# Moving the low-part subtraction of the second expert table's activations from GpSimd to VectorE

## The chip, the cores and the metric

The kernel runs on one core of a Trainium2 chip. The metric is the device time of one execution in microseconds (us), read as the median of several runs; smaller is better. The engines are named as the profile names them: PE (TensorE, matrix products; PEld is its weight load), DVE (VectorE), ACT (ScalarE), POOL (GpSimd) and SP (SyncE, which issues the bulk loads).

## What is computed

Two transformer blocks on 256 tokens of width 2048. The change lies in the last stage of the second block, a mixture of 16384 single-row experts:

```
act = gelu(einsum('cd,ckd->ck', hc, u_tab[ec])) * gate      # 128 picked experts a token
out = einsum('ck,ckd->cd', act, v_tab[ec])                  # sum of the picked rows of v_tab
return rmsnorm(x + out)
```

`u_tab` and `v_tab` are the first and the second table, 16384 rows of 2048 float32 values each.

## The kernel before

Almost all products are made in float32r from a high and a low part: with a = ah + al and v = vh + vl, a product is ah·vh + ah·vl + al·vh, three matmuls that accumulate in one PSUM bank. Where a table is streamed, `_stream` (lines 231 to 255) loads a piece, ACT rounds it to its high part (`hi`, line 251) and DVE subtracts that from the piece (`lo`, line 254). All matmuls go through `_mm`, line 259.

The expert stage is `_peer`. Its first part multiplies the tokens with every row of the first table and leaves, for every expert and token, the gated activation, zero where the expert was not picked. It lies in SBUF as 128 blocks (`sa` holds blocks 0 to 51, `sb` the rest), each 128 experts by 256 tokens. The ungated activations are also written to DRAM, into `wide`, beside 512 columns of the second table.

The second part, lines 1581 to 1604, is the stage of the change. It handles the 2048 output columns in two ways at once:

- Columns 0 to 1535 are done as a dense product, block by block. For each of the 128 blocks, ACT makes the high part of the activations (`ah`, line 1586) and an engine subtracts to get the low part (`al`, line 1587). The block's piece of the second table arrives in two loads, 512 KB and 256 KB, and is split into three groups of 512 columns (`hi` on ACT, `lo` on DVE). PE then does 18 matmuls a block: three groups, two halves of the tokens, and the three products hi·ah, lo·ah and hi·al, into six PSUM banks.
- Columns 1536 to 2047 are done by gathering. For each of the 128 picks of a token, and for each half of the tokens, `_row_sums` issues an indirect DMA on POOL (`vrow`, line 1454, 256 in all) that fetches, per token, 512 table values and 128 activations. DVE picks the right activation and multiplies it with the gate (line 1468, a SCALAR_TENSOR_TENSOR on 128x128 whose sum goes to `pval`), then adds the weighted row to two further PSUM banks (line 1475, a SCALAR_TENSOR_TENSOR on 128x512).

So one block asks of DVE three `lo`, two line-1468 and two line-1475 instructions; of ACT three `hi` and one `ah`; of POOL two gathers and one `al`; of PE 18 matmuls.

The order of instructions on each engine is made by a scheduler when the kernel is built, from the dependencies and from its own estimates; each engine then runs its list strictly in order. Buffers limit how far an engine can run ahead: `ah` and `al` have three each, `hi` and `lo` four each, `vrow` ten (five picks). An instruction that writes a buffer waits until the last reader of its former content is done.

Of the kernel before, what the change touches and what calls it, by code (L numbers as in the profile page):

```python
# [10 lines left out]
F32 = mybir.dt.float32  # L11
# [4 lines left out]
OP = mybir.AluOpType  # L16
# [214 lines left out]
def _stream(k, src, total):  # L231
    nc = k.nc
    for r in range(0, total, k.rk * 256):
        n = min(total - r, k.rk * 256)
        if k.raw2 is not None and n <= 512:
            raw = k.raw2.tile([128, 512], F32, name="raw")
        else:
            raw = k.raw.tile([128, k.rk * 256], F32, name="raw")
        small = k.n == 0
        if not small:  # L240
            load = nc.sync.dma_start(raw[:, :n], src[:, r:r + n])
            if k.side:
                _after(k, nc.sync.dma_start(*k.side.pop(0)), load)
        step = 512 if small else k.gr
        for a in range(0, n, step):
            m = min(step, n - a)
            if small:
                nc.sync.dma_start(raw[:, a:a + m], src[:, r + a:r + a + m])
            hi = k.hi.tile([128, k.gr], F32R, name="hi")
            lo = k.lo.tile([128, k.gr], F32R, name="lo")  # L250
            nc.scalar.activation(hi[:, :m], raw[:, a:a + m], AF.Copy)  # L251
            k.n += 1
            eng = nc.gpsimd if k.pool_lo and k.n % k.pool_lo == 0 else nc.vector
            k.low = eng.tensor_tensor(lo[:, :m], raw[:, a:a + m], hi[:, :m].bitcast(F32), op=OP.subtract)  # L254
            yield hi, lo, m


def _mm(k, out, lhsT, rhs, start=False, stop=False):
    return k.nc.tensor.matmul(out, lhsT, rhs, start=start, stop=stop, skip_group_check=True)  # L259
# [38 lines left out]
def _rsqrt(k, pool, v, n, tag):  # L298

    nc = k.nc  # L300
    y = pool.tile([128, n], F32, name="rs_y" + tag, tag="rs_y" + tag)
    t = pool.tile([128, n], F32, name="rs_t" + tag, tag="rs_t" + tag)
    yi = y.bitcast(I32)
    nc.vector.tensor_single_scalar(yi, v.bitcast(I32), 1, op=OP.logical_shift_right)
    nc.vector.tensor_scalar(yi, yi, -1, 0x5F3759DF, op0=OP.mult, op1=OP.add)
    for _ in range(3):
        nc.vector.tensor_tensor(t, y, y, op=OP.mult)
        nc.vector.scalar_tensor_tensor(t, t, -0.5, v, op0=OP.mult, op1=OP.mult)
        nc.vector.scalar_tensor_tensor(y, t, 1.5, y, op0=OP.add, op1=OP.mult)
    return y  # L310
# [1134 lines left out]
def _row_sums(k, picks, wide, rows, acc):  # L1445


    nc = k.nc
    ready = []

    def fetch(j):
        for t in range(2):
            r = rows.tile([128, DS + 128], F32, name="vrow")
            nc.gpsimd.indirect_dma_start(r, None, wide, bass.IndirectOffsetOnAxis(ap=picks.row[:, t, j:j + 1], axis=0),  # L1454
                                         element_offset=128 * t)
            ready.append(r)

    ahead = RB // 2 - 1
    for j in range(ahead):
        fetch(j)  # L1460
    for j in range(128):
        got = []
        for t in range(2):
            r = ready.pop(0)
            p, v = (r[:, DS:], r[:, :DS]) if t else (r[:, :128], r[:, 128:])

            w = picks.val[:, t, j:j + 1]
            i = nc.vector.scalar_tensor_tensor(p, p, picks.gate[:, t, j:j + 1], k.ident, op0=OP.mult, op1=OP.mult, accum_out=w)  # L1468
            _after(k, i, k.low)
            got.append((v, w))  # L1470
        for t, (v, w) in enumerate(got):
            if j == 0:
                i = nc.vector.tensor_scalar(acc[t], v, w, None, op0=OP.mult)
            else:
                i = nc.vector.scalar_tensor_tensor(acc[t], v, w, acc[t], op0=OP.mult, op1=OP.add)  # L1475
            _after(k, i, k.low)
        if j + ahead < 128:
            fetch(j + ahead)
        yield


def _peer(k, I, O, hctx, pers, sa, tctx, t1, x3n, wide, rb):
    nc, tc = k.nc, k.tc
# [20 lines left out]
    with ExitStack() as sctx:  # L1504
# [69 lines left out]
        with ExitStack() as c:  # L1574
            pso = c.enter_context(tc.tile_pool(name="pso", bufs=1, space=bass.MemoryType.PSUM))
            v2 = c.enter_context(tc.tile_pool(name="v2", bufs=3, side="right"))
            k.raw2 = c.enter_context(tc.tile_pool(name="raw2", bufs=6, side="right"))
            out = [[pso.tile([128, 512], F32, name=f"o{t}{q}") for q in range(4)] for t in range(2)]
            rows = c.enter_context(tc.tile_pool(name="vr", bufs=RB, side="right"))
            sums = _row_sums(k, picks, wide, rows, [out[t][3] for t in range(2)])  # L1580
            taken = 0
            for e in range(128):
                src = S_[0][:, e] if e < SA else S_[1][:, e - SA]
                ah = v2.tile([128, 256], F32R, name="ah")
                al = v2.tile([128, 256], F32R, name="al")
                nc.scalar.activation(ah, src, AF.Copy)
                nc.gpsimd.tensor_tensor(al, src, ah.bitcast(F32), op=OP.subtract)  # L1587
                for g, (vh, vl, _) in enumerate(_stream(k, I["v"][e], D - DS)):
                    for t in range(2):
                        ts = slice(t * 128, t * 128 + 128)  # L1590
                        for n, (s_, m_) in enumerate(((ah, vh), (ah, vl), (al, vh))):
                            _mm(k, out[t][g], s_[:, ts], m_, start=e == 0 and n == 0, stop=e == 127 and n == 2)
                if e == 24:

                    xn = [S_[0][:, 8 * t:8 * t + 8].rearrange("p a b -> p (a b)").rearrange("p (a b) -> p a b", b=512) for t in range(2)]
                    for t in range(2):
                        nc.scalar.dma_start(xn[t], x3n[t].rearrange("p (a b) -> p a b", b=512))
                while taken < 128 and taken * 122 < (e - 2) * 128:
                    next(sums, None)
                    taken += 1  # L1600
            for _ in sums:
                pass
            k.raw2 = None
            sctx.close()
            fin = c.enter_context(tc.tile_pool(name="fin", bufs=1))
            nf = fin.tile([128, 4, 512], F32, name="nf")
            nc.scalar.dma_start(nf.rearrange("p a b -> p (a b)"), I["normf"].to_broadcast([128, D]))
            for t in range(2):
                ss = fin.tile([128, 4], F32, name=f"ss{t}")
                sq = fin.tile([128, 512], F32, name=f"fsq{t}")  # L1610
                for q in range(4):
                    nc.vector.tensor_tensor(xn[t][:, q], xn[t][:, q], out[t][q], op=OP.add)
                    nc.scalar.activation(sq, xn[t][:, q], AF.Square, accum_out=ss[:, q:q + 1])
                v = fin.tile([128, 1], F32, name=f"fv{t}")
                nc.vector.tensor_reduce(v, ss, axis=AX.X, op=OP.add)
                nc.vector.tensor_scalar(v, v, 1.0 / D, EPS, op0=OP.mult, op1=OP.add)
                r = _rsqrt(k, fin, v, 1, f"f{t}")
                for q in range(4):
                    nc.vector.scalar_tensor_tensor(xn[t][:, q], xn[t][:, q], r, nf[:, q], op0=OP.mult, op1=OP.mult)
                    (nc.sync if q % 2 else nc.scalar).dma_start(O["out"][t * 128:t * 128 + 128, q * 512:q * 512 + 512], xn[t][:, q])  # L1620
# [47 lines left out]
def _second_block(k, I, O, hctx, cctx, x2d, sqa):  # L1668
# [20 lines left out]
    with ExitStack() as c:  # L1689
# [30 lines left out]
        _natural(k, xl, f, x3n)  # L1720
    cctx.close()
    _peer(k, I, O, hctx, pers, sa, tctx, t1, x3n, wide, rb)
    ctx.close()

# [42 lines left out]
```

## Time and profile before

| what | value |
| --- | --- |
| median of 3 runs | 3388.03 us (3386.93 to 3388.34) |
| the profiled execution's own time | 3391.95 us |
| its span in the profile | 3390.1 us |
| mean granted clock of PE | 0.983 |
| busy share of the span | PE 97%, DVE 76%, ACT 46%, POOL 26% |
| the stage of the change | 2778.76 to 3375.58 us of the span, first to last matmul |

The profile gives times from the start of the span. In a timeline view a row has the start, the duration, the engine, the line, the operation, what it writes and reads, and how many consecutive instructions were merged (x3); in brackets stands the time for which the engine sat idle before it and what it waited for. Rows of one engine can overlap by a few hundredths of a microsecond, since an instruction's end overlaps the next one's start; the distance between starts is therefore the cost of an instruction in a full engine. PE rows overlap much more, and the distance of starts is the only measure there.

### The profile page before, as it was taken

To read this page: it belongs to the slowest core of one execution; us is meant where nothing else is said; L and a number is where in the kernel's file an instruction comes from. 1 tells how busy PE (TensorE), PEld (TensorE's weight loads), DVE (VectorE), ACT (ScalarE), POOL (GpSimd) and SP (SyncE) were. 2 spreads that over 40 slices of the span, in tenths; PEclk is the share of its full clock that TensorE was granted. 3 is DMA by queue.
4 is the path that set the end of the run, shared out by engine and by line. 5 is a ranking of instruction groups with operands and counts; after the bars stand their busy time and mean duration, and the time that the engine had idled before them with its cause. 6 is when DMAs were issued, how large, how long until landed. Compare 5 with 4: busy or idle time off the path is not lost.

```text
span 3390.1 us, 65776 instructions
## 1 busy us (share of the span) xinstructions
PE 3272.4 (97%) x25018; PEld 3050.2 (90%) x25018; DVE 2571.7 (76%) x5477; ACT 1572.2 (46%) x2810; POOL 866.4 (26%) x1036
## 2 busy tenths in 40 slices
PE   8999899999999979999999999999999999999998
PEld 8999899999999979888879999999999996777776
DVE  8775587777744468788865778776777869999999
ACT  5444444444433345555454544444444444444444
POOL 3110210000000055454410000001223226666663
PEclk9999999999999979999989999999999999999999
DMA  5545455555555568653126566666566679999996
GB/s 194 168 156 174 131 168 186 178 184 187 182 180 186 172 248 286 194 169 100 52 81 200 181 200 195 190 200 188 179 176 183 180 218 335 316 320 324 317 324 225
DMA packets 239341, 680.46 MB, mean 201 GB/s; under 512 B 58160, under 2 KB 88752, under 8 KB 214832
## 3 DMA queue, kind: packets, MB, share of 16 engines
q1 hardware_dynamic: 167824, 560.53, 51.0%
q0 software_dynamic: 20480, 83.90, 7.5%
q10 hardware_dynamic: 50720, 31.82, 3.2%
q8 instruction: 196, 3.21, 0.4%
q14 instruction: 121, 0.99, 0.1%
HBM read 649.55 MB, written 60.16 MB: 209 GB/s over the span
## 4 chain that ended last, share of the span: by engine, by line
PE 71%; DVE 17%; DMA 7%; issue 3%; ACT 1%; POOL 1%; SPq 0%; DVEq 0%; ACTq 0%; POOLq 0%
PE acc L259 57%; DVE lo L254 6%; PE held L259 5%; DMA raw<-in_v 4%; DVE vrow L1468 3%; DVE o L1475 2%; PE o L259 2%; PE ps_g L259 2%; PE R L259 1%; DVE hl L349 1%; DVE ltmp L1038 1%; PE ps_p L259 1%; DMA wide<-in_vs 1%; DMA s<-g 1%; PE ps_S L259 1%
## 5 line engine op out<-in xcount | busy, mean ns | idle before, releaser
L251 ACT ACTIVATE hi<-raw 128x512 fp32r<-128x512 f32 (+1 forms) x1582 | 1147.4, 732 | 1365.3 <-PE acc L259 864.7
L254 DVE TENSOR_TENSOR lo<-raw,hi 128x512 fp32r<-128x512 f32 (+1 forms) x1492 | 1229.1, 841 | 574.2 <-ACT hi L251 561.5
L259 PE MATMUL acc<-hh,hi 128*128 128x256 f32 x4928 | 1406.6, 286 | 22.2 <-ACT hh L348 13.4
L259 PE MATMUL acc<-hh,lo 128*128 128x256 f32 x4928 | 1407.1, 286 | 13.3 <-DVE lo L254 13.1
L259 PE MATMUL acc<-hl,hi 128*128 128x256 f32 x4928 | 1400.2, 284 | 7.5 <-DVE hl L349 7.4
L259 PEld LDWEIGHTS acc<-hh,hi 128*128 128x128 f32 x4928 | 938.4, 190 | 26.0 <-ACT hh L348 14.2
L259 PEld LDWEIGHTS acc<-hh,lo 128*128 128x128 f32 x4928 | 932.0, 189 | 18.6 <-DVE lo L254 16.8
L259 PEld LDWEIGHTS acc<-hl,hi 128*128 128x128 f32 x4928 | 938.1, 190 | 11.0 <-DVE hl L349 9.7
L259 PE MATMUL o<-lo,ah 128*128 128x512 f32 x768 | 314.4, 410 | 13.2 <-DVE lo L254 7.2
L1454 POOL DMA_INDIRECT vrow<-wide,prow x256 | 269.6, 1053 | 198.2 <-DVE o L1475 146.9
L259 PE MATMUL o<-hi,al 128*128 128x512 f32 x768 | 304.3, 398 | 5.4 <-POOL al L1587 5.4
L259 PE MATMUL o<-hi,ah 128*128 128x512 f32 x768 | 222.7, 399 | 9.3 <-ACT hi L251 8.3
L259 PEld LDWEIGHTS o<-lo,ah 128*128 128x128 f32 x768 | 144.6, 188 | 85.4 <-DVE lo L254 55.1
L259 PE MATMUL acc<-gh,lo 128*128 128x256 f32 x704 | 199.2, 283 | 0.0
L259 PE MATMUL acc<-gl,hi 128*128 128x256 f32 x704 | 199.2, 283 | 0.0
L259 PE MATMUL acc<-gh,hi 128*128 128x256 f32 x704 | 199.2, 283 | 0.0
L259 PEld LDWEIGHTS o<-hi,ah 128*128 128x128 f32 x768 | 143.7, 189 | 49.4 <-ACT hi L251 14.7
L1525 POOL TENSOR_SCALAR oh<-iota,sel 128x128 f32<-128x128 f32 x128 | 92.9, 736 | 352.7 <-PE ps_g L259 323.7
L259 PEld LDWEIGHTS o<-hi,al 128*128 128x128 f32 x768 | 145.8, 190 | 36.6 <-POOL al L1587 5.8
L1475 DVE SCALAR_TENSOR_TENSOR o<-vrow,pval,o 128x512 f32<-128x512 f32 x254 | 178.3, 744 | 0.0
L254 POOL TENSOR_TENSOR lo<-raw,hi 128x512 fp32r<-128x512 f32 (+1 forms) x90 | 132.4, 1473 | 157.5 <-ACT hi L251 144.7
L1468 DVE SCALAR_TENSOR_TENSOR vrow<-vrow,pgate,ident 128x128 f32<-128x128 f32 x256 | 163.8, 675 | 2.4 <-DMA vrow<-wide,prow 2.4
(476 smaller groups left out, 4320.4 us busy)
## 6 DMA issues: line engine op xcount, KB each, us to landing
raw<-in_u SPq DMA_DIRECT2D x256, 512.0 KB, 4.5
raw<-in_w_up SPq DMA_DIRECT2D x85, 1024.0 KB, 5.1
raw<-in_v SPq DMA_DIRECT2D x128, 512.0 KB, 5.9
raw<-in_w_in SPq DMA_DIRECT2D x43, 1024.0 KB, 5.1
raw<-in_w_dn SPq DMA_DIRECT2D x40, 1024.0 KB, 4.9
wide<-in_vs SPq DMA_DIRECT2D x64, 512.0 KB, 6.0
raw<-in_v SPq DMA_DIRECT2D x128, 256.0 KB, 6.0
raw<-in_w_rkv SPq DMA_DIRECT2D x48, 512.0 KB, 3.8
```

What stands on the lines that cost most here:

```text
L251: nc.scalar.activation(hi[:, :m], raw[:, a:a + m], AF.Copy)
L254: k.low = eng.tensor_tensor(lo[:, :m], raw[:, a:a + m], hi[:, :m].bitcast(F32), op=OP.subtract)
L259: return k.nc.tensor.matmul(out, lhsT, rhs, start=start, stop=stop, skip_group_check=True)
L349: k.nc.vector.scalar_tensor_tensor(lo, t, scale, hi.bitcast(F32), op0=OP.mult, op1=OP.subtract)
L1038: nc.vector.tensor_tensor(tmp[:, :, 0:t], tt[:, :, 0:t], lq[:, 0:t, t][:, None, :].to_broadcast([128, 8, t]), op=OP.mult)
L1454: nc.gpsimd.indirect_dma_start(r, None, wide, bass.IndirectOffsetOnAxis(ap=picks.row[:, t, j:j + 1], axis=0), element_offset=128 * t)
L1468: i = nc.vector.scalar_tensor_tensor(p, p, picks.gate[:, t, j:j + 1], k.ident, op0=OP.mult, op1=OP.mult, accum_out=w)
L1475: i = nc.vector.scalar_tensor_tensor(acc[t], v, w, acc[t], op0=OP.mult, op1=OP.add)
L1525: eng.tensor_scalar(aj, iota, sel[:, 0, t:t + 1], None, op0=OP.is_equal)
```

## The change

One word: the subtraction that makes `al` is issued on DVE, not on POOL. Nothing else of the text changes.

```
@@ -1584,7 +1584,7 @@
                 ah = v2.tile([128, 256], F32R, name="ah")
                 al = v2.tile([128, 256], F32R, name="al")
                 nc.scalar.activation(ah, src, AF.Copy)
-                nc.gpsimd.tensor_tensor(al, src, ah.bitcast(F32), op=OP.subtract)
+                nc.vector.tensor_tensor(al, src, ah.bitcast(F32), op=OP.subtract)
```

The scheduler answers with other lists on four engines. On DVE, in the middle of the stage, the list of one block reads before as follows (`vrow_37796` and `vrow_37798` are the two gathered pieces of one pick, the `lo` are the three groups of one table block):

```order
L1468 SCALAR_TENSOR_TENSOR vrow_37796,pval_22307<-vrow_37796,pgate_22306,ident_58 128x128
L1468 SCALAR_TENSOR_TENSOR vrow_37798,pval_22307<-vrow_37798,pgate_22306,ident_58 128x128
L1475 SCALAR_TENSOR_TENSOR o03_34500<-vrow_37796,pval_22307,o03_34500 128x512
L1475 SCALAR_TENSOR_TENSOR o13_34504<-vrow_37798,pval_22307,o13_34504 128x512
L254 TENSOR_TENSOR lo_37991<-raw_37988,hi_37990 128x512
L254 TENSOR_TENSOR lo_38001<-raw_37988,hi_38000 128x512
L254 TENSOR_TENSOR lo_38013<-raw_38010,hi_38012 128x512
```

and with the change:

```order
L1468 SCALAR_TENSOR_TENSOR vrow_37796,pval_22307<-vrow_37796,pgate_22306,ident_58 128x128
L1468 SCALAR_TENSOR_TENSOR vrow_37798,pval_22307<-vrow_37798,pgate_22306,ident_58 128x128
L1587 TENSOR_TENSOR al_38031<-sb_27699,ah_38030 128x256
L1475 SCALAR_TENSOR_TENSOR o03_34500<-vrow_37796,pval_22307,o03_34500 128x512
L1475 SCALAR_TENSOR_TENSOR o13_34504<-vrow_37798,pval_22307,o13_34504 128x512
L254 TENSOR_TENSOR lo_37991<-raw_37988,hi_37990 128x512
L254 TENSOR_TENSOR lo_38001<-raw_37988,hi_38000 128x512
L254 TENSOR_TENSOR lo_38013<-raw_38010,hi_38012 128x512
```

The `al` of the block after the one whose `lo` follow stands between the two kinds of gather work; the rest keeps its order.

On POOL, at the start of the stage (the `sb` rows are the end of the part before, the DMA rows are the gathers), the list reads before:

```order
L1567 TENSOR_TENSOR sb<-sb,gtmp 128x512 x2
L1587 TENSOR_TENSOR al<-sa,ah 128x256 x3
L1567 TENSOR_TENSOR sb<-sb,gtmp 128x512
L1454 DMA vrow<-wide,prow 128x640 x10
L1587 TENSOR_TENSOR al<-sa,ah 128x256 x3
L1454 DMA vrow<-wide,prow 128x640 x4
L1587 TENSOR_TENSOR al<-sa,ah 128x256
L1454 DMA vrow<-wide,prow 128x640 x2
```

and with the change:

```order
L1567 TENSOR_TENSOR sb<-sb,gtmp 128x2x252
L1567 TENSOR_TENSOR sb<-sb,gtmp 128x512 x3
L1454 DMA vrow<-wide,prow 128x640 x256
L1763 UNCONDITIONAL_BRANCH
```

The `al` of blocks 3 to 5 stood behind ten gathers; now the 256 gathers follow each other alone.

On ACT, the `ah` of a block normally stands right before the three `hi` of the block ahead of it. At block 30 (counted from 0) the list before has two `ah` in a row, the second two blocks ahead:

```order
L1586 ACTIVATE ah_35852<-sa_20983 128x256
L1586 ACTIVATE ah_35898<-sa_20983 128x256
L251 ACTIVATE hi_35812<-raw_35810 128x512
L251 ACTIVATE hi_35822<-raw_35810 128x512
L251 ACTIVATE hi_35834<-raw_35832 128x512
```

and with the change:

```order
L1586 ACTIVATE ah_35852<-sa_20983 128x256
L251 ACTIVATE hi_35812<-raw_35810 128x512
L251 ACTIVATE hi_35822<-raw_35810 128x512
L251 ACTIVATE hi_35834<-raw_35832 128x512
L1586 ACTIVATE ah_35898<-sa_20983 128x256
```

The second `ah` has moved behind the three `hi`. The list before has eight blocks with an `ah` two ahead (12, 14, 19, 30, 50, 71, 91 and 111), the list with the change three (11, 14 and 19).

## Rows read from the trace of the kernel before

**Rows 1.** The page, part 1: busy time, share and instructions of each engine.

```profile
PE 3272.4 (97%) x25018; PEld 3050.2 (90%) x25018; DVE 2571.7 (76%) x5477; ACT 1572.2 (46%) x2810; POOL 866.4 (26%) x1036
```

**Rows 2.** Windows: length, busy of PE, PEld, DVE, ACT, POOL, clock, DMA share, GB/s.

```profile
2810.00:3350.00 540.00, 520.01 (x2107) 387.21 (x2106) 535.65 (x1081) 256.12 (x468) 344.80 (x359) 1.00 0.93 322
...
3050.00:3060.00 10.00, 10.00 (x44) 8.02 (x44) 9.67 (x20) 5.81 (x11) 7.31 (x8) 1.00 1.01 381
3060.00:3070.00 10.00, 10.00 (x45) 8.02 (x44) 10.00 (x20) 4.87 (x10) 6.57 (x8) 1.00 0.95 333
```

**Rows 3.** Timeline of DVE, 3055.5 to 3065: start, duration, engine, line, operation.

```profile
3055.56 1.22 DVE L1468 SCALAR_TENSOR_TENSOR vrow<-vrow,pgate,ident 128x128 f32<-128x128 f32 x1
...
3056.72 0.34 DVE L1468 SCALAR_TENSOR_TENSOR vrow<-vrow,pgate,ident 128x128 f32<-128x128 f32 x1
...
3058.31 1.88 DVE L254 TENSOR_TENSOR lo<-raw,hi 128x512 fp32r<-128x512 f32 x3
3060.11 1.23 DVE L1468 SCALAR_TENSOR_TENSOR vrow<-vrow,pgate,ident 128x128 f32<-128x128 f32 x1
```

**Rows 4.** Timeline of POOL beside it.

```profile
3055.88 0.75 POOL L1587 TENSOR_TENSOR al<-sb,ah 128x256 fp32r<-128x256 f32 x1
...
3059.27 1.14 POOL L1454 DMA_INDIRECT vrow<-wide,prow  x1 [0.30 <-DVE lo L254]
```

**Rows 5.** Timeline of DVE, 3036 to 3048.

```profile
3039.89 0.34 DVE L1468 SCALAR_TENSOR_TENSOR vrow<-vrow,pgate,ident 128x128 f32<-128x128 f32 x1
...
3040.43 1.40 DVE L1475 SCALAR_TENSOR_TENSOR o<-vrow,pval,o 128x512 f32<-128x512 f32 x2
...
3043.56 0.34 DVE L1468 SCALAR_TENSOR_TENSOR vrow<-vrow,pgate,ident 128x128 f32<-128x128 f32 x1
...
3047.23 0.34 DVE L1468 SCALAR_TENSOR_TENSOR vrow<-vrow,pgate,ident 128x128 f32<-128x128 f32 x1
```

**Rows 6.** Timeline of POOL beside it.

```profile
3040.87 0.75 POOL L1587 TENSOR_TENSOR al<-sb,ah 128x256 fp32r<-128x256 f32 x1
3041.78 1.49 POOL L1454 DMA_INDIRECT vrow<-wide,prow  x1 [0.16 <-issue]
```

**Rows 7.** Timeline of PE, 3040 to 3062: the same matmul of three blocks in a row.

```profile
3043.28 0.40 PE L259 MATMUL o<-lo,ah 128*128 128x512 f32 x1
...
3047.49 0.40 PE L259 MATMUL o<-lo,ah 128*128 128x512 f32 x1
...
3051.71 0.40 PE L259 MATMUL o<-lo,ah 128*128 128x512 f32 x1
```

**Rows 8.** Groups by form on DVE: count, busy us, mean ns, idle before.

```profile
L711 DVE TENSOR_TENSOR gl<-y,gh 128x256 fp32r<-128x256 f32 x44 | 18.4, 418 | 0.0
L349 DVE SCALAR_TENSOR_TENSOR hl<-x,cols,hh 128x256 fp32r<-128x256 f32 x64 | 44.1, 721 | 2.9 <-ACT hh L348 2.9
```

**Rows 9.** Timeline of PE: start of the stage.

```profile
2778.76 0.47 PE L259 MATMUL o<-hi,ah 128*128 128x512 f32 x1 [0.93 <-DVE gtmp L1561]
...
2783.32 1.26 PE L259 MATMUL o<-hi,ah 128*128 128x512 f32 x4 [1.53 <-ACT hi L251]
...
2801.68 2.93 PE L259 MATMUL o<-hi,al 128*128 128x512 f32 x6 [5.40 <-POOL al L1587]
```

**Rows 10.** Timeline of PE: end of the stage.

```profile
3375.18 0.40 PE L259 MATMUL o<-hi,al 128*128 128x512 f32 x1
```

**Rows 11.** Waits, 2778 to 2815: who waited for whom, us, times, longest.

```profile
DVE vrow L1468 <- DMA vrow<-wide,prow: 2.4, 3, 1.2
```

**Rows 12.** Timeline of PE, 2858 to 2872, where an `ah` is two ahead.

```profile
2864.04 0.39 PE L259 MATMUL o<-hi,al 128*128 128x512 f32 x1
2865.28 1.26 PE L259 MATMUL o<-hi,ah 128*128 128x512 f32 x4 [0.86 <-ACT hi L251]
```

**Rows 13.** Waits, 2800 to 3300.

```profile
ACT hi L251 <- DMA raw<-in_v: 3.4, 5, 0.8
```

More of the change, by code (lines that the diff above doesn't have):

```diff
@@ L1586, in _peer @@
                 nc.scalar.activation(ah, src, AF.Copy)
-                nc.gpsimd.tensor_tensor(al, src, ah.bitcast(F32), op=OP.subtract)
+                nc.vector.tensor_tensor(al, src, ah.bitcast(F32), op=OP.subtract)
                 for g, (vh, vl, _) in enumerate(_stream(k, I["v"][e], D - DS)):
```

## The prediction

> **What bounds the kernel now.** The page's first part says PE 97% and DVE 76% over the whole span [rows 1]. That average hides the stage in question, so the next view is the windows. From 2810 to 3350 us, DVE is busy 535.65 of 540 us, against 76% overall, and PE 520 of 540 [rows 2]. PE's busy time is no proof that PE is full, since its rows overlap; its pace must be taken from the distance of starts. So the reader should ask of this stage: how long is a block on DVE, how long on PE, and which of them sets the pace?
>
> For DVE I read its timeline. One block, from one first line-1468 instruction to the next, takes 3060.11 − 3055.56 = 4.55 us, with no idle time in it [rows 3]. The odd thing is the first of the two line-1468 instructions: it costs 3056.72 − 3055.56 = 1.16 us, and the second, the same shape and form, lasts 0.34. The POOL timeline shows what runs beside the long one: the `al` subtraction, 3055.88 to 3056.63 [rows 4]. A little earlier the same list runs differently: `al` at 3040.87 falls beside the line-1475 instructions, which stay at 1.40 for two [rows 5, 6], the line-1468 instructions are all 0.34, and a block takes 3043.56 − 3039.89 = 3.67 and 3047.23 − 3043.56 = 3.67 us [rows 5]. The difference between the two pictures is 0.88 us a block, and `al` on POOL is the only work that moved. So the `al` that POOL takes off DVE's hands costs DVE 0.88 us where it meets a line-1468 instruction.
>
> For PE, where nothing keeps it waiting, the same matmul of successive blocks starts at 3043.28, 3047.49 and 3051.71: 4.215 us a block for 18 matmuls [rows 7]. So DVE at 4.55 sets the pace now, PE at 4.215 is the next limit, 0.34 below.
>
> **The change part by part.** *DVE gains 128 subtractions of 128x256.* The nearest row is a subtraction of the same operands' kind and shape, 418 ns [rows 8]; in a full engine the next instruction starts a little before the end, three `lo` that last 1.88 take 3060.11 − 3058.31 = 1.80 [rows 3], so I take 418 less 80 ns, 0.34. The upper end is the 721 ns of a two-input instruction of this shape in the first block [rows 8], the lower end 0.30, half of a `lo`'s 0.60, since it has half the width.
>
> *DVE loses the stretch.* Nothing but the gathers is left on POOL in this stage. Gathers do not stretch DVE: a gather from 3041.78 to 3043.27 ran beside `lo` instructions in a block of 3.67 [rows 5, 6]. It is the gather that gets longer, 1.49 against 1.14 [rows 4, 6]. Two a block at 1.49 with 0.30 between are 3.6 us, still below 4.2, so POOL does not become the bound.
>
> The new DVE block is 3.67 + 0.34 = 4.01 us (3.97 to 4.39). With 4.01 the pace is PE's: 4.215.
>
> The Trainium skill (SBUF — State Buffer, Who interferes with whom) has a rule for this port: VectorE instructions with two SBUF inputs and GpSimd instructions that read SBUF exclude each other, and whichever starts first keeps the port while the other waits. The trace agrees with the exclusion, not with the order: the long line-1468 instruction starts 0.32 us before `al` and is the one that pays [rows 3, 4]. Taken by its letter the rule would leave DVE without loss in such a block, and the change would only add 128 × 0.34 = 44 us; I go by the rows.
>
> *What is queued behind the new instruction.* `al` waits on DVE for its `ah` and for a free `al` buffer, that is, for PE to finish the block three back. With PE at 4.215 a block and DVE at 4.01, DVE is ahead and will often wait there, about 0.2 us a block; behind it stand the line-1475 pair and the three `lo`. The `lo` have four buffers, more than a block's three, so PE has at least a group of prepared work, 4.215 / 3 = 1.4 us, when that happens; I cost it at nothing, and the cover is gone if a wait is longer than that.
>
> *The stage.* First matmul 2778.76, last 3375.18 + 0.40 [rows 9, 10]: 596.8 us for 128 blocks. At PE's pace they take 128 × 4.215 = 539.5. The gap is 57.3 us, and this is what stays of it:
> - the first wait for the table's load, 1.5 us [rows 9]: stays.
> - the start of the gathers: DVE waits 2.4 us in all for the first pieces [rows 11] with `lo` queued behind. Today it hides under the 5.4 us in which PE waits for `al` behind ten gathers [rows 9]. That wait goes with the change, so the 2.4 is late next. Between 0 and 2.4; I take 2.
> - the three blocks whose `ah` stands two ahead on ACT. There the `hi` of the next block wait for PE to finish the current one: starts 1.24 apart instead of 0.23 [rows 12], 1.0 us, with the `lo` behind it about 1.2: 3.5 us. Five others go.
> - late loads and other small waits: ACT waited 3.4 us in 500 for loads [rows 13], I take 1.5.
>
> Sum 8.5; saving 57.3 − 8.5 = 48.8 us. As a cross-check from the other side: about 100 blocks × 0.34 = 34, the 5.4 at the start, eight places × 1.2 = 10, together 49. The profiled execution took 3391.95, so it would take 3343.2; it lies 3.9 above the median of the runs, so the forecast is **3339 us**. Its own range is 3332 (only the 1.5 stays) to 3348 (all four items doubled).
>
> **The rivals.**
>
> *DVE still sets the pace, at a higher price of `al`.* If the subtraction costs 0.72, the block is 4.39: 128 × 0.175 = 22 us less gain, 3361. For it: a row with that mean exists. Against it: that row is of another operation (SCALAR_TENSOR_TENSOR) in another stage, and the subtraction of exactly this form took 418 ns.
>
> *The transfers become the bound.* The DMA engines are 0.93 busy at 322 GB/s now [rows 2]; with blocks of 4.215 instead of 4.55 the demand is 348 GB/s, a share of 1.00. Ten microseconds at 381 GB/s, at a share of 1.01, were reached [rows 2], so the share is not at its ceiling; but if the 333 GB/s of the next window is what can be kept up, a block takes 4.215 × 348/333 = 4.40 and the time is 3363.
>
> *Slower: the stretch is not `al`'s.* If the first line-1468 instruction is long by itself, say because it waits for its row or for a semaphore while counted as busy, then DVE keeps 4.55 and adds 0.34: 540 / 4.55 = 119 blocks × 0.34 = 40 us more, less the 5.4 of the start, 3423. This decides once a block on DVE with `al` in it exceeds 4.55, that is, if more than 0.54 of the 0.88 stays. For it: DVE is at 99% of this stretch and gets work. Against it: the clean blocks, where the same instructions with the same waits take 0.34 [rows 5]. The Trainium skill (Perfetto Trace Analysis, Optimizing Scalar/DVE Operations) advises to take work off a saturated VectorE, to ScalarE or even GpSimd, with the warning that for the last it might not help because of the shared port. Its first half speaks for this rival, and the clean blocks for the warning.
>
> *No difference.* The 256 gathers take over the collisions, stretching DVE by the 0.54 a block that would be gained at DVE's pace: 119 blocks stay at 4.55, only the 5.4 of the start goes, within 6 us of now. Against it stands the gather beside `lo` above.
>
> **How the numbers follow.** PE sets the pace: 0.75, around 3339. Dearer `al`: 0.08. Transfers: 0.08. No difference: 0.03. Slower: 0.04. The remaining 0.02 lie between 3364 and 3381. The range is 3331 to 3364: from PE's floor to the two rivals at 3361 and 3363. A measurement of this kernel tells about 0.2% (7 us) from no change. Faster by more: 0.75 + 0.08 + 0.08 + 0.02 = 0.93; within: 0.03; slower: 0.04.
>
> **What would show it.** In the changed kernel both line-1468 instructions of a block should last 0.34, `al` on DVE about 0.4, and DVE should show idle time again, in front of `al` or of `lo`, some 5% of the stage (0.2 of 4.215). The same matmul of successive blocks should start 4.2 us apart, and DMA should move near 350 GB/s. The wait of PE for `al` at the start should be gone, and three waits of PE for `hi` of about 1 us should be left. I am wrong if a line-1468 instruction of 1.2 us is still there, if DVE is without idle time, or if ACT waits for loads in every block.

## The result, and the profile after

| | time, us | against the kernel before, run beside it |
| --- | --- | --- |
| the change, first set | 3348.22 (3340.99 to 3351.88, 4 runs) | 0.9881 [0.9863, 0.9898] |
| the change, second set (after_again) | 3337.24 (3329.28 to 3340.22, 5 runs) | 0.9846 [0.983, 0.9862] |
| the change, third set (after_third) | 3344.13 (3339.18 to 3348.38, 4 runs) | 0.9858 [0.9843, 0.9873] |
| forecast | 3339 (3331 to 3364) | |

The kernel became faster, by 39.8, 50.0 and 46.8 us between the medians (the kernel before: 3387.97, 3387.27, 3390.96), where 49 was forecast. The profiled execution took 3346.89 us, its span 3345.1, with a granted clock of 0.986; against the profiled execution of before that is 45.1 us less.

The busy line of the page, then the chain of work that ended last by engine, both of the kernel after, and last the chain of the kernel before:

```profile
PE 3241.9 (97%) x25018; PEld 3053.5 (91%) x25018; DVE 2526.5 (76%) x5605; ACT 1573.1 (47%) x2810; POOL 763.9 (23%) x908
```

```profile
PE 85%; DVE 8%; DMA 4%; issue 1%; ACT 1%; POOL 0%; SPq 0%; ACTq 0%; DVEq 0%; POOLq 0%
```

```profile
PE 71%; DVE 17%; DMA 7%; issue 3%; ACT 1%; POOL 1%; SPq 0%; DVEq 0%; ACTq 0%; POOLq 0%
```

DVE has 128 instructions more than in [rows 1] and was busy 45 us *less*; POOL was busy 102 us less. The busy share of DVE over the span is 76% as before and tells nothing. The chain does: 14% of the span moved to PE, out of DVE, DMA and issue.

The windows (length, then busy time of PE, PEld, DVE, ACT, POOL, then the granted clock, the DMA share and GB/s) of the stage after, the full one and two pieces of its start:

```profile
2795.00:2800.00 5.00, 1.59 (x7) 0.99 (x6) 3.25 (x11) 0.94 (x2) 3.78 (x5) 0.84 1.00 388
2800.00:2805.00 5.00, 5.00 (x12) 3.89 (x13) 5.00 (x12) 0.63 (x1) 3.89 (x4) 0.50 0.90 297
...
2900.00:3300.00 400.00, 400.00 (x1709) 321.58 (x1708) 393.74 (x977) 209.45 (x380) 207.20 (x198) 1.00 0.97 352
```

From 2900 to 3300 us PE has no idle time at all, DMA moves 352 GB/s where [rows 2] had 322, at a share of 0.97. The two rows of the start show something else, and they are where the forecast was off; more below.

The timeline of DVE after, one block in the middle, and the same matmul group of two blocks in a row on PE:

```profile
3054.79 2.10 DVE L254 TENSOR_TENSOR lo<-raw,hi 128x512 fp32r<-128x512 f32 x3
3056.81 0.35 DVE L1468 SCALAR_TENSOR_TENSOR vrow<-vrow,pgate,ident 128x128 f32<-128x128 f32 x1
...
3057.35 0.42 DVE L1587 TENSOR_TENSOR al<-sb,ah 128x256 fp32r<-128x256 f32 x1
3057.69 1.41 DVE L1475 SCALAR_TENSOR_TENSOR o<-vrow,pval,o 128x512 f32<-128x512 f32 x2
3059.01 2.11 DVE L254 TENSOR_TENSOR lo<-raw,hi 128x512 fp32r<-128x512 f32 x3
3061.03 0.35 DVE L1468 SCALAR_TENSOR_TENSOR vrow<-vrow,pgate,ident 128x128 f32<-128x128 f32 x1
```

```profile
3043.62 1.10 PE L259 MATMUL o<-hi,ah 128*128 128x512 f32 x4
...
3047.84 1.10 PE L259 MATMUL o<-hi,ah 128*128 128x512 f32 x4
```

The 1.22 us of [rows 3] has become 0.35. `al` costs DVE 3057.69 − 3057.35 = 0.34 of distance. The block is 3061.03 − 3056.81 = 4.22 us, PE's own pace (4.22 there). The slack of DVE does not show as a wait: the three `lo` take 3056.81 − 3054.79 = 2.02 from start to start here and 1.80 in [rows 3], so 0.22 a block sits between them, in gaps that the overlapping row ends hide. A reader who looks for DVE's idle time in its busy share (98% in the windows) would call DVE full.

The start and the end of the stage on PE, after:

```profile
2777.44 0.47 PE L259 MATMUL o<-hi,ah 128*128 128x512 f32 x1 [0.93 <-DVE gtmp L1561]
...
2781.04 1.25 PE L259 MATMUL o<-hi,ah 128*128 128x512 f32 x4 [0.57 <-ACT hi L251]
...
2799.77 0.79 PE L259 MATMUL o<-lo,ah 128*128 128x512 f32 x1 [3.41 <-DVE o L1473]
...
2808.35 0.73 PE L259 MATMUL o<-hi,ah 128*128 128x512 f32 x2 [0.72 <-ACT hi L251]
...
2811.53 0.74 PE L259 MATMUL o<-hi,ah 128*128 128x512 f32 x2 [1.51 <-ACT hi L251]
...
3330.15 0.39 PE L259 MATMUL o<-hi,al 128*128 128x512 f32 x1
```

So the stage takes 3330.15 + 0.39 − 2777.44 = 553.1 us, against 596.8 before [rows 9, 10], 548 forecast and 539.5 at PE's pace. It also began 1.3 us earlier. The waits from 2778 to 2815 us, after (who waited for whom, us, times, longest), and below them one of the queue of the bulk loads, 2785 to 2812 us:

```profile
ACT hi L251 <- DMA raw<-in_v: 8.4, 3, 5.2
...
DVE vrow L1468 <- DMA vrow<-wide,prow: 5.2, 3, 3.3
```

```profile
SPq L241 <- DVE lo L254: 19.4, 6, 9.6
```

The wait of [rows 11] has grown from 2.4 to 5.2 us. The last line tells what hangs on it: a load overwrites a piece of the table that `lo` has read, so while DVE waits for gathers, with `lo` queued behind, SP waits too, here up to 9.6 us.

### The profile page after: what moved, and what is told of

It is laid out like the page before. It is cut to its first block, busy times and chain, and to the rows that moved or that the text cites. A ratio compares the mean times of both kernels' runs of the same rounds, so it can differ in the third digit from the quotient of the medians.

```text
span 3345.1 us, 65651 instructions
## 1 busy us (share of the span) xinstructions
PE 3241.9 (97%) x25018; PEld 3053.5 (91%) x25018; DVE 2526.5 (76%) x5605; ACT 1573.1 (47%) x2810; POOL 763.9 (23%) x908
## 4 chain that ended last, share of the span: by engine, by line
PE 85%; DVE 8%; DMA 4%; issue 1%; ACT 1%; POOL 0%; SPq 0%; ACTq 0%; DVEq 0%; POOLq 0%
PE acc L259 57%; PE o L259 15%; PE held L259 5%; PE ps_g L259 2%; DVE lo L254 1%; DVE ltmp L1038 1%; DVE hl L349 1%; PE R L259 1%; PE ps_p L259 1%; DMA wide<-in_vs 1%; PE ps_m L259 1%; DVE tt L1039 1%; DMA s<-g 0%; DVE x L676 0%; ACT hi L251 0%
## 5 line engine op out<-in xcount | busy, mean ns | idle before, releaser
L259 PE MATMUL acc<-hh,hi 128*128 128x256 f32 x4928 | 1405.3, 285 | 21.2 <-ACT hh L348 13.4
L259 PE MATMUL o<-lo,ah 128*128 128x512 f32 x768 | 305.6, 398 | 3.4 <-DVE o L1473 3.4
L254 POOL TENSOR_TENSOR lo<-raw,hi 128x512 fp32r<-128x512 f32 (+1 forms) x90 | 132.5, 1475 | 157.0 <-ACT hi L251 142.1
```

## The experiments

The theory on trial: `al` on POOL stretches a DVE instruction beside it, and without it PE sets the pace. The rivals: that instruction is long by itself; POOL disturbs DVE whatever it does; and after the change the transfers or DVE, not PE, are the bound.

"Stage" is the time from the first to the last matmul of the second-table stage in the profiled execution, as above; 128 blocks at PE's pace of 4.215 are 539.5 us.

### Is it the POOL subtraction that stretches DVE?

**pool_twin.** The change, with a second subtraction left on POOL in each block, into a block of activations that nobody reads any more:

```
                nc.vector.tensor_tensor(al, src, ah.bitcast(F32), op=OP.subtract)
+                if e > 0 and e != SA:
+                    ax = S_[0][:, e - 1] if e < SA else S_[1][:, e - SA - 1]
+                    nc.gpsimd.tensor_tensor(ax, src, ah.bitcast(F32), op=OP.subtract)
```

> The changed kernel, with a second subtraction of the same operands on GpSimd in each block (126 in all), whose result goes to a block of activations that nobody reads any more. Theory (a GpSimd instruction that reads SBUF holds up a VectorE instruction with two SBUF inputs beside it): the stretch comes back, a block on VectorE takes 4.01 + 0.88 = 4.89 us, VectorE sets the pace again, 3348 + 126 x 0.67 = about 3432 us (3405 to 3440, since some will fall beside the line-1475 pair), and line-1468 or lo instructions of over 1.1 us are in the trace. Rival (the gain came from the order: al no longer queued behind the gathers, fewer blocks with an ah two ahead): nothing waits for the second subtraction, so the time stays at 3341 to 3352.

Measured: 3401.73 us (3396.42 to 3406.93, 10 runs), 1.0034 [1.0024, 1.0043] of the kernel before, slower than it. The timelines of DVE and, below it, POOL:

```profile
3101.61 0.34 DVE L1468 SCALAR_TENSOR_TENSOR vrow<-vrow,pgate,ident 128x128 f32<-128x128 f32 x1
...
3105.61 1.23 DVE L1468 SCALAR_TENSOR_TENSOR vrow<-vrow,pgate,ident 128x128 f32<-128x128 f32 x1
...
3110.51 1.22 DVE L1468 SCALAR_TENSOR_TENSOR vrow<-vrow,pgate,ident 128x128 f32<-128x128 f32 x1
```

```profile
3099.80 0.74 POOL L1590 TENSOR_TENSOR sb<-sb,ah 128x256 f32<-128x256 f32 x1 [0.50 <-DVE o L1475]
...
3105.93 0.75 POOL L1590 TENSOR_TENSOR sb<-sb,ah 128x256 f32<-128x256 f32 x1
...
3110.81 0.76 POOL L1590 TENSOR_TENSOR sb<-sb,ah 128x256 f32<-128x256 f32 x1
```

The block without a POOL subtraction beside line 1468 takes 3105.61 − 3101.61 = 4.00 us, the next, with one at 3105.93, 4.90. Nobody reads what that instruction makes, so the 0.90 is no wait for data. The time lies a little under the expected range, since not every block collides: the mean of line 1468 is 616 ns between 2850 and 3300 us, where one of 1.23 and one of 0.34 in each block would be 785.

**pool_memset.** The change, with a POOL instruction that only writes, 128x1024 in each block:

```
+                if e >= 4 and not SA <= e < SA + 4:
+                    ax = S_[0][:, e - 4:e] if e < SA else S_[1][:, e - SA - 4:e - SA]
+                    nc.gpsimd.memset(ax, 0.0)
```

> The changed kernel, with a memset of 128x1024 on GpSimd in each block, into four blocks of activations that nobody reads any more: GpSimd writes SBUF and reads none. Theory with the read side as the shared part: VectorE is not stretched, line-1468 instructions stay at 0.35 and lo at 0.68, 3341 to 3355 us. Rival (any GpSimd work beside VectorE stretches it by its own length): some 0.3 to 0.9 us a block more on VectorE, of which 0.2 is hidden behind TensorE, 3360 to 3430 us.

Measured: 3339.21 us (3338.75 to 3343.42, 4 runs), 0.9854 [0.9837, 0.987], 1.8 under the expected range. The groups by form on POOL and DVE, 2850 to 3300 us (count, busy us, mean ns, idle before), then a memset and what DVE did beside it:

```profile
L1590 POOL MEMSET sb<- 128x1024 f32 x70 | 67.0, 957 | 48.6 <-DVE al L1587 47.4 <-issue 0.9
```

```profile
L1468 DVE SCALAR_TENSOR_TENSOR vrow<-vrow,pgate,ident 128x128 f32<-128x128 f32 x222 | 68.3, 345 | 0.0
```

```profile
2899.24 0.97 POOL L1590 MEMSET sa<- 128x1024 f32 x1
```

```profile
2899.66 1.88 DVE L254 TENSOR_TENSOR lo<-raw,hi 128x512 fp32r<-128x512 f32 x3
```

The 345 ns do not settle the question by themselves: no memset of this stretch fell beside a line-1468 instruction, most fell beside line 1475. The `lo` settle it. They have two SBUF inputs as well, and a subtraction on POOL makes one of them last up to 1.63 us in the kernel before; here 39 `lo` have a memset beside them for more than 0.15 us, and they last 0.68 us in the mean and 0.69 at most, as elsewhere. So POOL work that is longer than `al` (957 ns against 0.75 us) costs such an instruction nothing when it reads nothing, and it is not POOL being busy that stretches. For line 1468 itself this is an inference from `lo`.

**pool_one_input.** The change, with a POOL multiplication of one input instead:

```
+                if e > 0 and e != SA:
+                    ax = S_[0][:, e - 1] if e < SA else S_[1][:, e - SA - 1]
+                    nc.gpsimd.tensor_scalar(ax, src, 1.0, None, op0=OP.mult)
```

> The changed kernel with one more GpSimd instruction per block, a multiplication by 1 with one SBUF input of 128x256 into a dead block of activations, where pool_twin had a subtraction with two inputs and pool_memset a write alone. Theory (it is GpSimd's reading from SBUF that collides with a VectorE instruction of two SBUF inputs, one input being enough): line 1468 is again 0.9 to 1.3 us where the multiplication falls beside it, its mean is 0.45 us or more, and the time is 3365 to 3405. Rival (only a GpSimd instruction with two inputs collides): line 1468 stays at 0.35 and the time is that of the changed kernel, 3335 to 3352.

Measured: 3342.40 us (3337.60 to 3344.44, 4 runs), 0.9862 [0.9845, 0.9878]; the time is the rival's. For line 1468 it still tells neither apart, as the timelines show, DVE above and POOL below:

```profile
3101.15 2.08 DVE L254 TENSOR_TENSOR lo<-raw,hi 128x512 fp32r<-128x512 f32 x3
3103.16 0.34 DVE L1468 SCALAR_TENSOR_TENSOR vrow<-vrow,pgate,ident 128x128 f32<-128x128 f32 x1
```

```profile
3101.18 1.36 POOL L1590 TENSOR_SCALAR sb<-sb 128x256 f32<-128x256 f32 x1
```

The multiplication settled beside the `lo`, not beside line 1468: it had ended at 3102.54, 0.62 us before line 1468 began, and so it went in almost every block: of the 224 line-1468 instructions from 2850 to 3300 us two have it beside them, at 0.34 and 0.49 us. The `lo` tell more: of 148 with a multiplication beside them 91 last 0.67 to 0.70 us and 57 last 0.85 to 0.93. So one input on POOL costs a `lo` at most a quarter of a us, and the 0.2 us a block that the `lo` have to give away hide most of it in the time. What it would cost line 1468 stays open.

**pool_timed.** The kernel before, with `al` on POOL as it was, but made to wait for the second line-1468 instruction of the previous pick:

```
...
             _after(k, i, k.low)
+            k.pick = i
...
-                nc.gpsimd.tensor_tensor(al, src, ah.bitcast(F32), op=OP.subtract)
+                i = nc.gpsimd.tensor_tensor(al, src, ah.bitcast(F32), op=OP.subtract)
+                if k.pick is not None:
+                    k.tc.add_manual_dep(i.ins, k.pick.ins.name, SYNC, reason="beside the row sums")
```

> The kernel before, with al on GpSimd, but each al waits for the second line-1468 instruction of the pick before it, so that it runs beside the line-1475 pair, which has only one SBUF input. Theory: no stretch, a block on VectorE takes 3.67 us, TensorE sets the pace at 4.215; the eight blocks with an ah two ahead are as before and the start is as before (al behind ten gathers), so 3388 less about 118 x 0.34 = 40: 3340 to 3360 us. Rival (the gain came from moving al off GpSimd and out of its queue): al is on GpSimd as before, so 3380 to 3395 us.

Measured: 3347.82 us (3346.26 to 3352.37, 4 runs), 0.9878 [0.9861, 0.9895]. POOL's and DVE's timelines:

```profile
3102.60 0.74 POOL L1590 TENSOR_TENSOR al<-sb,ah 128x256 fp32r<-128x256 f32 x1 [1.05 <-DVE vrow L1469]
```

```profile
3101.80 0.35 DVE L1469 SCALAR_TENSOR_TENSOR vrow<-vrow,pgate,ident 128x128 f32<-128x128 f32 x1
...
3102.35 1.41 DVE L1477 SCALAR_TENSOR_TENSOR o<-vrow,pval,o 128x512 f32<-128x512 f32 x2
```

(Two lines were added above, so 1469 and 1477 are the lines 1468 and 1475 of the other kernels.) This is the strongest of the four: the same `al` on the same engine, 0.80 us behind the start of the block's gather work instead of 0.32 [rows 3, 4], and the time is 41.7 us under the kernel before (3389.54), with an extra wait in the program. The instruction beside which it now falls is not stretched, 1.41 for two as in [rows 5]. Taking `al` off POOL was never needed for that part; it must only not fall beside line 1468 or `lo` (13 `lo` beside it still last 1.04 us in the mean).

The forms fit. Line 1468 and `lo` have two SBUF inputs, line 1475 one from SBUF and one from PSUM. In the timelines of before from 2850 to 3330 us, taking rows of one line-1468 instruction, of three `lo` and of two line-1475 instructions that overlap an `al` by more than 0.15 us: 90 line-1468 instructions with a mean of 1.22 us against 0.34 for the 127 others; ten groups of three `lo` at 2.65 against 1.88; and eight pairs of line 1475 at 1.40 against 1.40. The Trainium skill (SBUF — State Buffer, Who interferes with whom) says the same: VectorE instructions with two SBUF inputs contend with GpSimd's reads, those with at most one do not, outside VectorE's two-port modes, and GpSimd instructions that only write do no harm. The three counts agree, and so does the memset beside `lo`. Its sentence on order, that whoever issues first holds the port, does not fit the rows: line 1468 starts 0.32 us before the subtraction here too (3105.61 and 3105.93) and is the one that is long. Spans of POOL are rough, so the true order stays open.

### What sets the pace after the change?

**dve_twin.** The change, with a second, unread subtraction on DVE behind `al`:

```
+                if e > 0 and e != SA:
+                    ax = S_[0][:, e - 1] if e < SA else S_[1][:, e - SA - 1]
+                    nc.vector.tensor_tensor(ax, src, ah.bitcast(F32), op=OP.subtract)
```

> The changed kernel with a second, unread subtraction of the same shape in each block on VectorE, right behind `al`. Theory (PE at 4.215 us a block sets the pace after the change, VectorE is close behind): the changed kernel's VectorE is busy 483.05 us of 495 in about 117.4 blocks, 4.11 us a block, so one more at 0.34 to 0.42 makes 4.45 to 4.53 us and VectorE sets the pace again; (4.45 to 4.53 - 4.215) x 128 = 30 to 40 us over the changed kernel's 3348, less up to 3.5 since no `ah` stands two ahead in this version: 3375 to 3388, and PE is to show idle time in every block. That is still at or below the 4.55 us that the same subtraction costs on GpSimd by way of the stretch. Rival A (VectorE has room for it, idle 5% as forecast): 0.20 us of it hide, 3360 to 3374. Rival B (the transfers, not PE, set the pace after the change): 3344 to 3352, since VectorE's work would hide behind them.

Measured: 3356.84 us (3353.51 to 3358.65, 4 runs), 0.9906 [0.989, 0.9921]; the change, run beside it, 3337.24. All three expectations missed. The sign and the place are the theory's (DVE sets the pace again, 19.6 us slower than the change), the size is not. DVE's timeline:

```profile
3101.61 0.45 DVE L1468 SCALAR_TENSOR_TENSOR vrow<-vrow,pgate,ident 128x128 f32<-128x128 f32 x1
...
3105.95 0.46 DVE L1468 SCALAR_TENSOR_TENSOR vrow<-vrow,pgate,ident 128x128 f32<-128x128 f32 x1
...
3110.29 0.46 DVE L1468 SCALAR_TENSOR_TENSOR vrow<-vrow,pgate,ident 128x128 f32<-128x128 f32 x1
```

The rows last some 0.1 us longer than the change's 0.35, and so do those of the other DVE instructions, with POOL doing nothing but gathers; no run here shows why. A block with one more subtraction is 4.34 us, not 4.45 to 4.53. The mistake was to take DVE's busy time over the number of blocks (4.11) for what a block costs: it holds the hidden gaps between the `lo`. The distance of starts, 4.01 + 0.34, would have given 4.35, and (4.35 − 4.215) × 128 = 17 us.

**less_pe.** The change, with two products instead of three in the third group, so 16 matmuls a block:

```
-                        for n, (s_, m_) in enumerate(((ah, vh), (ah, vl), (al, vh))):
-                            _mm(k, out[t][g], s_[:, ts], m_, start=e == 0 and n == 0, stop=e == 127 and n == 2)
+                        q = ((ah, vh), (ah, vl), (al, vh))[:2 if g == 2 else 3]
+                        for n, (s_, m_) in enumerate(q):
+                            _mm(k, out[t][g], s_[:, ts], m_, start=e == 0 and n == 0, stop=e == 127 and n == len(q) - 1)
```

> The changed kernel with the third product (`al` with the high part of the row sums) left out for the third group of 128 output rows and columns: 16 instead of 18 matmuls a block, so that part of the output lacks it. Theory (PE sets the pace): PE needs 4.215 x 16/18 = 3.75 us a block, VectorE 4.01 to 4.11 sets the pace, 128 x 0.10 to 0.20 = 13 to 26 us less than the changed kernel's 3348: 3322 to 3335, with the transfers at 357 to 366 GB/s. Rival (the transfers at 351 GB/s and 0.97 busy are the bound): no gain, 3344 to 3352.

Measured: 3319.76 us (3317.12 to 3323.74, 5 runs), 0.9798 [0.9785, 0.9811]; 17.5 less than the change beside it, and 2.2 under the expected range. DVE's timeline, and a window:

```profile
3097.52 0.35 DVE L1468 SCALAR_TENSOR_TENSOR vrow<-vrow,pgate,ident 128x128 f32<-128x128 f32 x1
...
3101.53 0.35 DVE L1468 SCALAR_TENSOR_TENSOR vrow<-vrow,pgate,ident 128x128 f32<-128x128 f32 x1
...
3105.53 0.35 DVE L1468 SCALAR_TENSOR_TENSOR vrow<-vrow,pgate,ident 128x128 f32<-128x128 f32 x1
```

```profile
2900.00:3300.00 400.00, 390.91 (x1567) 287.11 (x1568) 400.00 (x1002) 206.92 (x392) 227.49 (x194) 1.00 0.96 351
```

With matmuls taken away the time falls, so PE was the bound and the transfers were not: from 2850 to 3250 us they moved 361 GB/s here, more than the change's 352 (the 351 of the window shown holds fewer gathers). DVE is next, with a block of 4.01 and 4.00 us: the forecast's 4.01, seen here bare. The mean is a little higher, 400 / (1567 / 16) = 4.08, because a block in which two picks fall has 1.86 us more (0.55 for two line-1468 and 1.31 for two line-1475 instructions).

### Where does the change still lose against PE's pace?

**late_sums.** The change, with the picks taken later:

```
-                while taken < 128 and taken * 122 < (e - 2) * 128:
+                while taken < 128 and taken * 119 < (e - 6) * 128:
```

> The changed kernel, with the row sums started four blocks later (the test for taking a pick is taken x 119 < (e - 6) x 128), so that VectorE meets the first gathered rows after they have landed; the list on ScalarE then has no block with an ah two ahead. Theory (what was mis-sized is the start: VectorE waits in order for the first gathers with lo behind, TensorE waits 3.4 us and runs at half clock for a while, the loads slip behind): the 5 us more than forecast go, and the 3.5 us of the three blocks too, 3338 to 3343 us, with a narrower spread than 3341 to 3352. Rival (the excess is spread over the stage, from late transfers at 351 GB/s): 3345 to 3352 us as now.

Measured: 3334.20 us (3330.98 to 3335.63, 5 runs), 0.9836 [0.9823, 0.985], 3.8 under the lower edge of what was expected. PE's rows with a wait from the start of the stage on, all of them, and the last matmul; then a window of its start:

```profile
2773.23 0.47 PE L259 MATMUL o<-hi,ah 128*128 128x512 f32 x1 [0.93 <-DVE gtmp L1561]
...
2776.80 1.26 PE L259 MATMUL o<-hi,ah 128*128 128x512 f32 x4 [0.53 <-ACT hi L251]
...
3313.70 0.39 PE L259 MATMUL o<-hi,al 128*128 128x512 f32 x1
```

```profile
2794.00:2799.00 5.00, 5.00 (x23) 3.94 (x23) 2.02 (x4) 1.64 (x4) 1.67 (x2) 1.00 1.02 400
```

The stage is 540.9 us, PE's floor with 1.4 to spare. Its DVE list has 24 `lo` ahead of the first line-1468 instruction where the change has 12, so the gathers land while DVE has other work. The edit does a second thing: as expected, no block has an `ah` two ahead any more, and the three waits of PE that came with them are gone too.

**late_again and after_third.** The same version and the change on one chip. 

> The later row sums once more, now beside the changed kernel on the same chip. Theory (the start of the stage is what the changed kernel still loses; with later sums the stage is PE's floor): stage 540 to 542 us, that is 8 to 13 us below the changed kernel's of the same call, and the time lower by as much, give or take what lies ahead of the stage. Rival (the 3334 measured before was the chip or the spread, not the edit): within 3 us of the changed kernel's time, and a stage of 547 us or more.

> The changed kernel a third time, beside the two versions with later row sums, so that they share a chip and the runs of the kernel before. From its two sets so far (3341 to 3352, then 3329 to 3340): 3335 to 3350, with the second-table stage at 549 to 554 us; what its executions differ by beyond that is to lie ahead of this stage.

Measured: 3330.70 us (3329.14 to 3336.18, 5 runs), 0.982 [0.9806, 0.9833], with later sums; 3344.13 for the change. The stages are 541.2 and 555.4 us. So the 13.4 us between the medians are the edit's (8 to 13 were expected), of which the three `ah` are about 2.9 (lead_one below), and this is the fastest version that computes everything. The stage of the change is 1.4 over what was expected of it: PE waited 3.22 us there and then once more, 4.12 for `hi`.

**lead_one.** The change, with the order on ACT fixed so that no `ah` stands two ahead:

```
...
-                nc.scalar.activation(ah, src, AF.Copy)
+                i = nc.scalar.activation(ah, src, AF.Copy)
+                if e > 2:
+                    _after(k, i, highs[e - 2])
...
+                highs.append(k.high)
```

(`k.high` is the last `hi` instruction that `_stream` issued.)

> The changed kernel with one order fixed on ScalarE: no `ah` is made before the second `hi` back, so that it never stands two blocks ahead. Theory of the forecast (three blocks with `ah` two ahead cost 1.2 us each): 3.5 us less than the changed kernel, 3344 to 3346, beside it in the same call. Rival (these waits hide in the start of the stage, where the gathers' first pieces are late anyway): the same within 1.5 us as the changed kernel, and the waits of PE at the first blocks are the same in length.

Measured: 3334.70 us (3332.84 to 3338.22, 5 runs), 0.9844 [0.9831, 0.9858]. The whole set lies below the 3344 to 3346, as the change's own second set does; beside that, the difference is 2.5 us (stage 547.1 against 550.0). The ranges of the two overlap, so the medians alone would not show it; the rows do. The change has a row with an idle time of 0.79 or 0.80 at each of the three blocks, here the first two of the second set:

```profile
2818.50 1.25 PE L259 MATMUL o<-hi,ah 128*128 128x512 f32 x4 [0.79 <-ACT hi L251]
...
2832.26 1.25 PE L259 MATMUL o<-hi,ah 128*128 128x512 f32 x4 [0.79 <-ACT hi L251]
```

In lead_one there is no such row. The waits at the start, 3.28 us for the first gathers, are untouched.

**after_again.** The change once more, on the chip of dve_twin, less_pe and lead_one.

> The changed kernel once more, to see how far its times spread and how much of the spread lies ahead of the second-table stage: 3341 to 3352, with the start of that stage (its first matmul) between 2771 and 2779 us and the stage itself 545 to 554 us long.

Measured: 3337.24 us (3329.28 to 3340.22, 5 runs), 3.8 under the lower edge of what was expected; the stage fits. It starts at 2772.93 us, 4.5 earlier than in the first profile, and takes 550.0 instead of 553.1. The code ahead of the stage is the same in all versions, and their profiles put its first matmul between 2768.91 (pool_one_input) and 2778.76 (before): up to 10 us between two executions lie there. What the rest of the 11 us between the first two medians is, no profile here tells.

**timed_late.** pool_timed with the later sums:

```
-                while taken < 128 and taken * 122 < (e - 2) * 128:
+                while taken < 128 and taken * 119 < (e - 6) * 128:
```

> The kernel before with `al` on GpSimd, each made to wait for the second line-1468 instruction of the previous pick (as in pool_timed), and with the later row sums. Theory (the collision is the whole loss on VectorE, and the rest is the start): PE's floor here too, stage 540 to 545 us and 3330 to 3340. Rival (GpSimd is the wrong engine for `al` at the start of the stage, behind the gathers, whenever the sums begin): the 5.3 us wait of PE stays and the time is 3343 to 3350.

Measured: 3350.10 us (3348.06 to 3353.10, 4 runs), 0.9875 [0.986, 0.989]. The theory missed. The time is at the upper edge of the rival's range, the rival's wait is there, and PE's row shows it:

```profile
2800.79 2.93 PE L260 MATMUL o<-hi,al 128*128 128x512 f32 x6 [5.35 <-issue]
```

Its `al` still stands behind ten gathers on POOL, whenever the sums begin. The stage is 558.0 us, as with the early sums (559.5): apart from this wait of PE, eight waits for `hi` add up to 6.8 us in its view of waits. So the move to DVE, with the orders on POOL and ACT that came with it, buys something beyond the collision: `al` no longer stands behind the first gathers, and five of the eight `ah` two ahead are gone.

## Why the prediction was right, and where it was off

- **The stretch is `al`'s.** Right. A POOL subtraction that nobody reads brings it back, an `al` on POOL at another time does not. Forecast 0.88 a block, 0.90 in pool_twin. With that, the slower rival falls (the long line-1468 instruction is not long by itself), and so does "no difference": from 2850 to 3300 us, with the gathers still on POOL, 223 line-1468 instructions have a mean of 347 ns.
- **The new DVE block is 4.01.** Right: 4.01 and 4.00 where DVE sets the pace (less_pe), `al` at 0.34 of distance. The rival with a dearer `al` falls.
- **PE at 4.215 sets the pace.** Right: no idle time on PE from 2900 to 3300 us, and fewer matmuls make it faster.
- **The transfers.** That rival falls: 352 GB/s were kept up for 400 us, 400 for five.
- **What stays at the start.** Here the sum was off. The forecast left 8.5 us over PE's floor; 13.6 are there (553.1 − 539.5). The step that failed is the item "the start of the gathers", priced "Between 0 and 2.4; I take 2". Its upper bound was the wait for the first pieces in the trace of before. It was 5.2 on DVE here, and PE sat idle for 3.41 and lost 3.6 (3.8 between two starts, less 0.23). The second part was missing from the sum: behind that idle time PE ran at the lower of its two clock levels, 0.50 in the windows, 1.2 instead of 2.4 GHz, for the 12 matmuls from 2799.77 to 2805.05, 5.28 instead of 12 × 0.234 = 2.8. That is 2.5 more, 6.1 in place of 2. In the trace of before the same level follows the wait of 5.40 (the x6 of [rows 9] takes 2.93), and I had read that row for its idle time alone. A third part was missing as well, the loads held up behind the same wait; it is the last of the next items.
- **The other items** were sized well enough: the first table load 0.7 for 1.5; the three `ah` two ahead 0.96 each (starts 1.19 apart instead of 0.23), 2.9 for 3.5, which lead_one gave back; late loads about 2.6 for 1.5, behind the one load for which ACT waited 5.2 us. With the 6.1 these make 12.3 of the 13.6. That load is no item of its own: SP issued it at 2801.27 us, 0.03 after a `lo` had ended and 10 us after the load before it. In late_sums, where DVE waits for no gather, PE has no such wait, so most of the 2.6 belongs to the start of the gathers too: nearer 8.7 than 2.
- **DVE's idle time** was forecast in front of `al` or `lo`, 5% of the stage. It is between the `lo`, 0.22 of 4.22 in such a block, and the busy share shows only 1.6% of it.
- **Two readings.** The cross-check counted all eight places with an `ah` two ahead as gained, where the sum let three of them stay; with five it gives 34 + 5.4 + 6 = 45 us, nearer to the stage's 43.7 than the 48.8 of the sum. And the gather of 1.14 us lay beside a `lo` like that of 1.49, so the two rows do not show what `lo` does to a gather; that gathers leave DVE as it is does stand, by the 347 ns above.
- **The number.** For the profiled execution the sum gave 3343.2, and it took 3346.9: 5.1 more in the stage, less the 1.3 by which the stage began earlier. The 3.9 then taken off for the median of the runs had no cause behind them but what executions differ by: the execution profiled here lies 1.3 under its set's median. The three sets have medians of 3337, 3344 and 3348. That the forecast of 3339 lies among them is in part luck: the first set is 9 above it, and the sets differ by more than the start was mis-sized by.

## What to carry to other kernels

Before an instruction is moved off GpSimd because VectorE "has no room", or onto it because it has, look for VectorE instructions with two SBUF inputs that are longer than their twins, and see what GpSimd reads beside them: here one moved subtraction cost 0.34 and gave back 0.88. The first proof is cheap: shift the GpSimd instruction in time and leave it where it is. When a bound moves to the next engine, what remains is often at the start of the stage, where transfers first land in front of an engine that works in order: put work ahead of the first wait (here 12 more `lo` ahead, with three `ah` in better places, were worth some 13 us), and price an idle time of PE with the slow matmuls behind it.

## What the runs showed of the hardware that was not expected

- PE's lower level followed idle times of 3.41 (12 slow matmuls) and also 2.48 us (pool_memset, clock 0.50 in the three microseconds behind it), and not those of 1.47 us (dve_twin) and 1.73 us (pool_twin), with clock 1.00 behind both.
- A POOL memset of 0.96 us leaves a `lo` beside it at 0.68 us; a POOL subtraction of 0.75 us with two reads costs a DVE instruction of 0.34 us another 0.88; a POOL multiplication with one read makes some `lo` 0.2 us longer.
- The first gathers of the stage were issued at about the same time, at 2787.59 us before and 2787.42 after. DVE stood ready for the first piece at 2793.38 before and 2791.19 after, and waited 2.4 us in all before and 5.2 after.
